# Dividing the inverse's PSUM copies of a delta-rule layer between ScalarE and VectorE

## The chip, the core and the metric

The kernel runs on one core of a Trainium2 chip, in one launch. The core has five engines that take their instructions strictly in order from a queue of their own: TensorE (PE in the profile, with its weight loads shown apart as PEld), VectorE (DVE), ScalarE (ACT), GpSimd (POOL) and SyncE (SP, which here only issues DMAs). Engines wait for each other by semaphores. The metric is the device time of the launch in microseconds (us); the kernel before takes 1310.35 us (median of 3 runs, 1309.5 to 1310.55).

## The reference: what is computed

The model is a two-layer encoder on 512 tokens of width 1024: layer 0 mixes tokens by a bidirectional gated delta rule (8 heads, keys and values of 128, chunks of 64 tokens), layer 1 by gated linear attention, and each is followed by a LayerNorm, an MLP with a squared ReLU and another LayerNorm. The change is in layer 0 alone. For each head, direction and chunk of 64 tokens the reference solves a triangular system:

```
kb = k * beta[..., None]
a_mat = where(strict, einsum('bhncd,bhnsd->bhncs', kb, k) * decay_mat, 0.0)
lhs = a_mat + eye(CHUNK)
sol = triangular_solve(lhs, rhs, lower=True, unit_diagonal=True)
u, w = sol[..., :dv], sol[..., dv:]
```

and then runs a recurrence over the chunks of the head (`v_new = u - w @ state`, output, new state), whose output is normed, gated and multiplied with the output weights.

## The kernel before, in words

The 512 tokens make four blocks of 128 (NT = 4), each holding two chunks; with two directions there are eight 128x128 matrices per head (U = 8). They are inverted all together, by joining blocks of growing size. `solve` (line 1593) first inverts 4x4 diagonal blocks, then walks through the sizes 4, 8, 16, 32 and 64. At each size there are three groups of eight float16 matmuls into PSUM tiles called `lv` (`prod`, line 1677): first ath by Dd (the off-diagonal blocks times the inverse so far); the result is copied, masked to the blocks in question, into the zeroed tile `pz` of that size; then Xd by pz, and pz by Xd, whose results update the inverse `Dd` and its transpose `Xd`. "Both factors" are these two. `d` counts the directions; a block of direction 0 and one of direction 1 lie in different rows (PSUM partitions) of the same `lv` tile, and one `lv` tile fills one PSUM bank. For sizes 4, 8 and 16 one VectorE product with a mask makes `pz`. For size 32 it is four ScalarE copies of 32x128 (line 1696). For size 64 `pz` is one ScalarE and one VectorE instruction (lines 1712 and 1710), and then two ScalarE copies write the last block of Dd (line 1717) and two VectorE copies the last block of Xd (line 1719).

After it one Newton step refines the inverse (tiles `nw`, lines 1728 to 1751), which gives `xf`. `recur` (line 1755) then runs the recurrence over four steps: matmul pairs `m` (line 1776) alternate with small ScalarE and VectorE instructions (tiles `r`, `vd`, `vn`, `sn`), and the head ends with 14 output matmuls `op` (line 1812). `finish` (line 1817) squares `op` on ScalarE (`junk`), makes a reciprocal root (`rsy`, `rst`, `ors`), scales (`fo`), transposes on TensorE (`otp`) and makes `p`, and its two halves `oh` and `ol`, the input of the output product.

Three heads are in work at once: the loop in `gdn` (line 1359) traces `recur` of head i-2, `solve` of head i-1, `project` of head i (96 matmuls of 512 columns, tiles `pjk`, `pjq`, `pjv`, `pjz`) and `finish` of head i-2. When no head is left to project, the output product of heads 0 to 5 (`out_pieces`, tiles `oa`, 144 matmuls of 512 columns) takes the projections' place, and `out_last` (line 315; tiles `ob`) adds heads 6 and 7: for each of four token blocks and two halves of the columns a product with the identity in full float32 (line 332) that brings in the residual, three matmuls for head 6 and three for head 7. When both halves of a block are complete, its LayerNorm (`layernorm`, line 223) runs on VectorE, and then its transposes (`tp`, line 190), which the first products of the MLP (`pj`) need.

The order in which these pieces stand in each engine's queue is not written by hand: the framework's scheduler puts them there when the program is built, by priority (mostly the order of the trace) and by its own estimate of what is ready at what time. It also sets the semaphores. So a change of a few copies can move instructions in all queues. `self.next.solved`, the last copy into Dd, is the instruction behind which the next head's exponentials `E` (line 1617) are allowed.

## Time and profile before

| | |
|---|---|
| median of 3 runs | 1310.35 us (1309.5 to 1310.55) |
| the profiled execution, its own time | 1310.2 us |
| its span (first to last instruction) | 1308.5 us |
| TensorE busy | 1289.2 us, 99% |
| VectorE busy | 1106.3 us, 85% |
| ScalarE busy | 804.4 us, 61% |
| granted TensorE clock | 0.996 |
| stage with the changed copies | from 60 to 363 us of the span (first and last of them at 73.8 and 363.3 us) |
| end of the last head's `op` matmuls | 383.5 us |
| LayerNorm of layer 0 and its transposes | to about 420 us |

A row of the timeline names the start, the duration, the engine, the line, the operation, the tiles (out<-in) and the shape, and in brackets the engine's idle time before it and who ended it. A matmul's duration is modelled and covers its pipeline, so what a matmul costs a busy TensorE is the distance between the starts of two matmuls that follow each other. A full-precision float32 matmul stands as two rows.

### The profile page before, as it was taken

The numbers are of one execution on the slowest core, as the hardware profiler recorded it, in microseconds if no ns is written. First come the engines' busy times: TensorE is split into PE (matmuls) and PEld (weight loads), VectorE is DVE, ScalarE is ACT, GpSimd is POOL, SyncE is SP. The second block draws the span as 40 slices with busy tenths as digits, with TensorE's granted clock in tenths as the row PEclk, the third lists the DMA queues.
The fourth block names the chain that finished last, engine by engine and source line by source line (L and its number), as shares of the span: only waits on it lengthen the run. The fifth ranks groups of instructions, "written<-read, shape, count | busy, mean of one in ns | idle before, by whom it ended". The sixth has DMA issues, their size and how long they took to land.

```text
span 1308.5 us, 22228 instructions
## 1 busy us (share of the span) xinstructions
PE 1289.2 (99%) x8586; PEld 1106.7 (85%) x8586; DVE 1106.3 (85%) x1795; ACT 804.4 (61%) x1604; POOL 134.5 (10%) x190
## 2 busy tenths in 40 slices
PE   8999999999999999999999999999999999999996
PEld 7778888888878899999998888888888899999985
DVE  7888887988868998999989697877888789989987
ACT  5767776677543656666657754564456566666656
POOL 5000000000003710101102100000001001101021
PEclk9999999999999999999999999999999999999998
DMA  5333313233332665566657421211317276556565
GB/s 192 98 107 97 98 57 107 81 114 104 107 113 82 177 175 167 122 198 162 179 146 156 136 97 62 68 64 50 107 54 228 78 210 164 144 176 139 170 143 144
DMA packets 47805, 165.92 MB, mean 127 GB/s; under 512 B 5923, under 2 KB 6611, under 8 KB 47699
## 3 DMA queue, kind: packets, MB, share of 16 engines
q1 hardware_dynamic: 33603, 114.52, 25.8%
q0 software_dynamic: 13984, 49.95, 18.8%
q8 instruction: 67, 1.10, 0.3%
q14 instruction: 39, 0.32, 0.1%
q10 hardware_dynamic: 112, 0.03, 0.0%
HBM read 125.00 MB, written 2.65 MB: 98 GB/s over the span
## 4 chain that ended last, share of the span: by engine, by line
PE 92%; DVE 3%; ACT 2%; DMA 1%; issue 1%; SPq 0%; DVEq 0%; ACTq 0%
PE pjv L128 3%; PE pjv L129 3%; PE pjv L130 3%; PE pX L130 3%; PE pX L129 3%; PE fx L130 3%; PE fx L128 3%; PE fx L129 3%; PE pX L128 3%; PE m L1776 3%; PE fyz L130 3%; PE fyz L128 3%; PE fyz L129 3%; PE pY L129 2%; PE pY L130 2%; PE pY L128 2%
## 5 line engine op out<-in xcount | busy, mean ns | idle before, releaser
L102 ACT CAST wh<-wst 128x1024 fp32r<-128x1024 f32 x151 | 158.5, 1050 | 104.6 <-PE fyz L129 28.3
L107 DVE TENSOR_TENSOR wl<-wst,wh 128x1024 fp32r<-128x1024 f32 x149 | 183.1, 1231 | 40.6 <-ACT wh L102 40.5
L107 DVE TENSOR_TENSOR w2l<-w2r,w2h 128x1024 fp32r<-128x1024 f32 x92 | 111.4, 1221 | 20.5 <-ACT w2h L102 20.5
L102 ACT CAST w2h<-w2r 128x1024 fp32r<-128x1024 f32 x94 | 98.4, 1048 | 41.5 <-DMA w2r<-w2r 22.9
L415 POOL DMA_DIRECT2D w2r<-w2r x56 | 47.9, 887 | 492.9 <-DVE w2l L107 387.7
L464 DVE TENSOR_TENSOR wst<-wst 128x512 f32<-128x512 f32 x120 | 79.9, 686 | 0.8
L102 ACT CAST ah<-h 128x1024 fp32r<-128x1024 f32 x56 | 58.8, 1050 | 30.6 <-PE pY L129 11.9
L107 DVE TENSOR_TENSOR al<-h,ah 128x1024 fp32r<-128x1024 f32 x56 | 68.3, 1220 | 6.6 <-ACT ah L102 6.6
L130 PE MATMUL pX<-w2h,al 128*128 128x512 f32 x168 | 66.3, 394 | 0.0
L129 PE MATMUL pX<-w2l,ah 128*128 128x512 f32 x168 | 65.9, 392 | 0.0
L128 PE MATMUL pX<-w2h,ah 128*128 128x512 f32 x168 | 65.4, 390 | 0.0
L128 PE MATMUL pjv<-wh,xth 128*128 128x512 f32 x128 | 54.7, 428 | 0.0
L130 PE MATMUL fyz<-xh,wl 128*128 128x256 f32 x192 | 53.5, 278 | 0.0
L130 PE MATMUL fx<-xth,wl 128*128 128x256 f32 x192 | 53.4, 278 | 0.0
L128 PE MATMUL fyz<-xh,wh 128*128 128x256 f32 x192 | 53.4, 278 | 0.0
L128 PE MATMUL fx<-xth,wh 128*128 128x256 f32 x192 | 53.2, 277 | 0.0
L130 PE MATMUL fx<-xh,wl 128*128 128x256 f32 x192 | 53.2, 277 | 0.0
L129 PE MATMUL fx<-xtl,wh 128*128 128x256 f32 x192 | 53.2, 277 | 0.0
L129 PE MATMUL fyz<-xl,wh 128*128 128x256 f32 x192 | 53.1, 277 | 0.0
L129 PE MATMUL fx<-xl,wh 128*128 128x256 f32 x192 | 53.1, 277 | 0.0
L128 PE MATMUL fx<-xh,wh 128*128 128x256 f32 x192 | 53.1, 277 | 0.0
L129 PE MATMUL pj<-xtl,wh 128*128 128x256 f32 (+1 forms) x160 | 52.0, 326 | 0.2 <-DVE xtl L194 0.2
(542 smaller groups left out, 4315.4 us busy)
## 6 DMA issues: line engine op xcount, KB each, us to landing
wst<-in_w SPq DMA_DIRECT2D x68, 512.0 KB, 4.8
w2r<-in_w SPq DMA_DIRECT2D x60, 512.0 KB, 4.5
w2r<-w2r POOLq DMA_DIRECT2D x56, 512.0 KB, 5.9
wst<-in_a_in SPq DMA_DIRECT2D x31, 512.0 KB, 3.8
wst<-in_b_vr SPq DMA_DIRECT2D x16, 512.0 KB, 3.3
wst<-in_a_out SPq DMA_DIRECT2D x8, 512.0 KB, 4.7
wst<-in_b_in SPq DMA_DIRECT2D x8, 512.0 KB, 3.4
wst<-in_b_out SPq DMA_DIRECT2D x8, 512.0 KB, 3.2
```

What stands on the lines that cost most here:

```text
L102: h = nc.scalar.copy(hi, src)
L107: self.halves = h, nc.vector.tensor_tensor(lo, src, hi.bitcast(F32), ALU.subtract)
L128: mm(ps, ah, bh, start=start, stop=False, **kw)
L129: mm(ps, ah, bl, start=False, stop=False, **kw)
L130: self.last_mm = mm(ps, al, bh, start=False, stop=stop, **kw)
L415: nc.gpsimd.dma_start(blocks[a + (q,)], blocks[b + (q,)], accum_op=ALU.add)
L464: plus = lambda a, b: V.tensor_tensor(a, a, b, ALU.add)
L1776: T.matmul(ps[:, d, :], *ops(d), start=True, stop=True)
```

## The change

At size 32 the two copies of direction 1 stay on ScalarE and the two of direction 0 go to VectorE. In the last block each factor gets one copy on each engine: Dd's direction 0 on ScalarE and direction 1 on VectorE, Xd's direction 0 on VectorE and direction 1 on ScalarE. Counted per head, the 32x128 copies are four on ScalarE before and two on each engine now; the 64x256 copies are two on each engine before and now, but in other pairs. `self.next.solved` becomes the first of the four, ScalarE's copy into Dd.

```
@@ -1693,8 +1693,9 @@
                 for d in (1, 0):
                     for b in range(2):
                         r0, c0 = 64 * b + s * (1 - d), 64 * b + s * d
-                        A.copy(pd[r0:r0 + s, dirs[d], c0:c0 + s],
-                               ps.rearrange("p d (n b) s -> p d n b s", n=NT)[r0:r0 + s, d, :, b, :])
+                        (A.copy if d else V.tensor_copy)(
+                            pd[r0:r0 + s, dirs[d], c0:c0 + s],
+                            ps.rearrange("p d (n b) s -> p d n b s", n=NT)[r0:r0 + s, d, :, b, :])
@@ -1713,10 +1714,11 @@
         ps = prod(xd, pd, 64, 0)
         px = prod(pd, xd, 64, 1)
-        for d in range(2):
-            self.next.solved = A.copy(dd[row(1 - d), dirs[d], row(d)], ps[row(1 - d), d, :, :])
-        for d in range(2):
-            V.tensor_copy(xd[row(d), dirs[d], row(1 - d)], px[row(d), d, :, :])
+        where = lambda t, i, d: (t[row(i), dirs[d], row(1 - i)], (px if t is xd else ps)[row(i), d, :, :])
+        self.next.solved = A.copy(*where(dd, 1, 0))
+        V.tensor_copy(*where(dd, 0, 1))
+        V.tensor_copy(*where(xd, 0, 0))
+        A.copy(*where(xd, 1, 1))
```

The new lines push what follows down by one or two: L1717 and L1719 of before are L1718 to L1721 now, L1728 is L1730, L1776 is L1778, L1812 is L1814, L1834 is L1836. The multiset of instructions stays the same but for the engine of these copies; the queues from about 430 us of the span on are the same. Three places show what moved. The semaphores that an instruction waits for stand in brackets.

The first place is VectorE's queue at the last block of head 7, the last head (Xd and Dd are the two factors, `a` is what the Newton step makes of `nw`, `z` the residual). Before:

```order
L1710 TENSOR_SCALAR pz_146<-lv 64x4x64 [waits Activation_49]
L311 SCALAR_TENSOR_TENSOR z<-z,oa 128x512 [waits DMAHW4_49,PE_49]
L1719 CAST Xd<-lv 64x4x64 [waits PE_49]
L1719 CAST Xd<-lv 64x4x64
L1840 SCALAR_TENSOR_TENSOR p<-otp,ng,sil 128x512 [waits PE_49]
```

Now:

```order
L1711 TENSOR_SCALAR pz_146<-lv 64x4x64 [waits Activation_49]
L1720 CAST Xd<-lv 64x4x64 [waits DVE_49,PE_49]
L1719 CAST Dd<-lv 64x4x64 [waits Activation_49]
L311 SCALAR_TENSOR_TENSOR z<-z,oa 128x512 [waits DMAHW7_49,PE_49]
L1732 SCALAR_TENSOR_TENSOR a_4969<-nw,Dd 128x512 [waits PE_49]
```

VectorE's copy into Dd waits for a ScalarE instruction ("Activation"), the copy into the other half of Dd, and stands behind the copy into Xd. The two copies at size 32 (L1696) on VectorE wait for ScalarE in the same way in all eight heads.

The second place is TensorE's queue in the last head's recurrence, from one `m` pair to the end of `op` and on to the first transpose of `finish`. Before (of the 14 `op` matmuls the first eleven are left out, and the `ob` groups that follow, up to `otp`, too):

```order
L1776 MATMUL m_5205<-r,xf 128x128 x2
L129 MATMUL oa<-wl,oh_340 128x512
L130 MATMUL oa<-wh,ol 128x512
L128 MATMUL oa<-wh,oh_340 128x512
L1776 MATMUL m_5216<-vd,kt 128x128 x2
...
L1812 MATMUL op<-vn,qke 128x128 x2
L1812 MATMUL op<-sn,qd 128x128
L129 MATMUL oa<-wl,oh_341 128x512
L130 MATMUL oa<-wh,ol 128x512
L128 MATMUL oa<-wh,oh_342 128x512
```

Now:

```order
L1778 MATMUL m_5205<-r,xf 128x128 x2
L332 MATMUL ob<-z,ident 128x512
L1778 MATMUL m_5216<-vd,kt 128x128 x2
...
L1814 MATMUL op<-vn,qke 128x128 x2
L1814 MATMUL op<-sn,qd 128x128
L128 MATMUL ob<-oah,oh_343 128x512
L129 MATMUL ob<-oal,oh_343 128x512
L130 MATMUL ob<-oah,ol 128x512
L1836 MATMUL otp<-ident,fo 128x128 x4
L128 MATMUL ob<-oah,oh_343 128x512
```

The `oa` matmuls that stood between the `m` pairs are used up, and pieces of `ob` stand there. Before, 8 `oa` matmuls, three `ob` products with the identity and 6 other `ob` matmuls stand between the last `op` and the first `otp`; now 3 `ob` matmuls. Counted over the whole stage, 880 of the 888 matmuls of 512 columns (projections and `oa`) stood ahead of the end of the last head's `op`, and none of `ob`; now all 888 do, and five products with the identity and 12 other `ob` matmuls. Changes from a group of float16 matmuls to one of 512 columns number 107 before and 118 now, up to the first `tp`.

The third place is ScalarE's queue behind the last head's recurrence (`vn` its last values, `junk` the squares of `op`, `wh` halves of the MLP's weights, `rsy` and `fo` as above). Before:

```order
L1794 ACTIVATE vn<-m_5230 128x128 x2
L1824 ACTIVATE junk,oss<-op 128x128 x2
L102 CAST wh<-wst 128x1024
L1824 ACTIVATE junk,oss<-op 128x128
L102 CAST wh<-wst 128x1024
L1824 ACTIVATE junk,oss<-op 128x128
L202 ACTIVATE rsy<-oss,bias_77 128x4
```

Now:

```order
L1796 ACTIVATE vn<-m_5230 128x128 x2
L1826 ACTIVATE junk,oss<-op 128x128 x4
L202 ACTIVATE rsy<-oss,bias_77 128x4
L203 ACTIVATE rsy<-rsy 128x4
L1832 ACTIVATE fo<-op,ors 128x128 x4
```

Two weight casts that stood between the squares now stand ahead of `vn`, and VectorE's subtractions that go with them likewise.

## The prediction

> **What bounds the kernel now.** I read the first part of the page first, then the copies by tile, then the timeline around them.

> ```profile
> span 1308.5 us, 22228 instructions
> PE 1289.2 (99%) x8586; PEld 1106.7 (85%) x8586; DVE 1106.3 (85%) x1795; ACT 804.4 (61%) x1604; POOL 134.5 (10%) x190
> ```

> TensorE is busy for 99% of the span. A copy on another engine can cost or save time only where TensorE waits for it, or where it changes what TensorE has left to do while it waits for something else. The view of the `lv` tile gives the copies (minimum/median/maximum in ns, first and last start):

> ```profile
> L1696 ACT CAST pz<-lv x32: 247/256/258, 73.8 to 359.0; 32x128 f16<-32x128 f32 x32
> L1717 ACT CAST Dd<-lv x16: 365/366/367, 78.9 to 363.1; 64x256 f16<-64x256 f32 x16
> L1719 DVE CAST Xd<-lv x16: 407/422/428, 79.7 to 363.3; 64x256 f16<-64x256 f32 x16
> ```

> Around the first head's copies the timeline (start, duration, engine, work) shows how much of them TensorE sees:

> ```profile
> 73.76 1.07 ACT L1696 CAST pz<-lv 32x128 f16<-32x128 f32 x4 [1.33 <-PE lv L1682]
> 73.78 0.48 PE L129 MATMUL pjk<-xtl,wh 128*128 128x512 f32 x1
> 74.10 0.40 PE L130 MATMUL pjk<-xth,wl 128*128 128x512 f32 x1
> 74.46 0.48 PE L128 MATMUL pjk<-xth,wh 128*128 128x512 f32 x1
> 74.88 0.28 PE L1682 MATMUL lv<-pz,Xd 128*128 128x64 f16 x4
> 78.87 0.76 ACT L1717 CAST Dd<-lv 64x256 f16<-64x256 f32 x2 [0.96 <-PE lv L1682]
> 79.21 0.40 PE L130 MATMUL pjq<-xth,wl 128*128 128x512 f32 x1
> 79.68 0.22 PE L1728 MATMUL nw<-Dd,ath 128*128 128x128 f16 x1
> ```

> While ScalarE makes its four copies (1.07 us), TensorE multiplies for the projections. A matmul of 512 columns occupies it for 0.23 us (383.80 to 384.03 in the rows further down), so the product at 74.88, 0.42 behind its forerunner, waited 0.19 us for `pz`; the one at 79.68, 0.47 behind, waited 0.24 us for Dd. Of this kind there are six waits for the first (1.2 us in all) and eight for the second (2.0 us). All that faster copies could give is these **3.2 us**; everything else of ScalarE's 14.1 us of copies (32 by 0.256 and 16 by 0.366) is hidden behind projections, and later `oa`.

> **The copies themselves.** Two of four small copies and one of two large ones change engine. VectorE's 32x128 cast is not in the trace. It lies between ScalarE's own 0.256 us and VectorE's 64x256 at 0.422; the work is a quarter, so I take a value near the lower end, 0.29. For the 64x256 copies both engines have rows: 0.366 and 0.422. If both engines worked side by side, four copies of 1.07 us would become two by 0.29, and the waits above would vanish: −3.2 us. But the program as built makes VectorE's copy wait for ScalarE's, since both read the same `lv` tile. Whether such a wait costs its full length, the kernel before shows in size 64, where `pz` is already divided in just this way:

> ```profile
> 361.12 0.38 ACT L1712 ACTIVATE pz<-lv 64x256 f16<-64x256 f32 x1 [1.85 <-PE lv L1682]
> 361.53 0.42 DVE L1710 TENSOR_SCALAR pz<-lv 64x256 f16<-64x256 f32 x1
> ```

> VectorE begins 0.03 us after ScalarE's end: one behind the other, never together. By that, two ScalarE copies and then two on VectorE take about 0.53 + 0.03 + 0.58 = 1.14 us, against 1.07: no gain, +0.07. At the last block a gain is left: Dd's first copy on ScalarE and Xd's on VectorE read different tiles, so the two engines overlap across the factors, and both factors are done in about 0.85 us instead of 0.37 × 2 for Dd and then 0.87 from 79.73 for Xd. Dd, which `nw` needs, is complete after 0.37 + 0.03 + 0.42 = 0.82 instead of 0.76 (+0.06), unless VectorE is held in Xd's copy. The eight waits for Dd I count as staying or going by what stands ahead of them in TensorE's queue: where fillers are moved there, they go. The whole sum of waits removed is taken as −2.0, between 0 and −3.2.

> [...]

> **What waits behind the wait.** VectorE takes its queue in order, so in each head two of its new copies hold it until ScalarE is done: 16 times, 0.3 to 0.5 us by the durations above, 5 to 8 us of VectorE over a stage of 300 us in which it is 85% busy (page). What queues behind (the V casts, `ktp`, the residual) feeds TensorE with some slack; the order has also 11 more changes from float16 to 512 columns (107 to 118), and the first matmul after such a change takes 0.32 instead of 0.23 us (383.48 to 383.80 to 384.03): 11 × 0.09 = +1.0. For the shorter covers of `pz` at size 64 and `ktp` I add +0.9, an estimate from five places with 0.2 us each, as in the wait at 74.88. Together with −2.0: **−0.1**, between −3.2 and +2.

> **The order, where the money lies.** With the inverse later in the plan, the `oa` matmuls are used up early. In the last head TensorE has 8 more of them, 5 products with the identity and 12 other `ob` ahead of the last `op`. What stood behind `op` before:

> ```profile
> 383.34 0.39 PE L1812 MATMUL op<-sn,qd 128*128 128x128 f32 x2
> 383.48 0.48 PE L129 MATMUL oa<-wl,oh 128*128 128x512 f32 x1
> 383.80 0.39 PE L130 MATMUL oa<-wh,ol 128*128 128x512 f32 x1
> 384.03 0.39 PE L128 MATMUL oa<-wh,oh 128*128 128x512 f32 x1
> ...
> 385.41 1.02 PE L332 MATMUL ob<-sil,ident 128*128 128x512 f32 x2
> 385.87 0.79 PE L128 MATMUL ob<-oah,oh 128*128 128x512 f32 x1
> 386.50 0.39 PE L129 MATMUL ob<-oal,oh 128*128 128x512 f32 x1
> ...
> 389.66 0.33 PE L1834 MATMUL otp<-ident,fo 128*128 128x128 f32 x1
> ...
> 391.79 0.50 PE L128 MATMUL ob<-oah,oh 128*128 128x512 f32 x1
> ```

> An identity product with the matmul behind it spans 385.41 to 386.50, so the product itself is 1.09 − 0.23 = 0.86. Moved ahead of the end of `op`: 8 × 0.23 + 5 × 0.86 + 12 × 0.23 = 1.84 + 4.30 + 2.76 = **8.9 us**; the last `op` ends about 8.9 − 0.1 = 8.8 us later. That alone would be no loss, since what went ahead is not to be done behind. It is a loss as far as the stretch behind is bound by something else than TensorE, and it is: `finish` needs ScalarE and VectorE before `otp`, and after `oh` the LayerNorm needs VectorE.

> ```profile
> 384.43 1.04 ACT L102 CAST wh<-wst 128x1024 fp32r<-128x1024 f32 x1
> 385.63 1.04 ACT L102 CAST wh<-wst 128x1024 fp32r<-128x1024 f32 x1
> 387.31 1.22 DVE L107 TENSOR_TENSOR wl<-wst,wh 128x1024 fp32r<-128x1024 f32 x1
> 387.76 0.21 ACT L203 ACTIVATE rsy<-rsy 128x4 f32<-128x4 f32 x1
> 388.45 0.15 DVE L204 TENSOR_TENSOR rst<-rsy 128x4 f32<-128x4 f32 x1
> ```

> From the last `op` (383.48) to `otp` (389.66) the chain took 6.18 us. The two casts stood between the squares and held it by about 0.95 each (1.04 less the overlap of its ends), and the subtraction at 387.31 held `rst` by 0.4 (388.45, where 0.21 after 387.76 would be about 388.0). Both stand earlier now: 6.2 − 1.9 − 0.4 = 3.9. From there to the first `ob` with the new `oh` 391.79 − 389.66 = 2.13. Then the LayerNorm; the stretches from there (their columns: window, length, then busy time of PE, PEld, DVE, ACT and POOL with counts):

> ```profile
> 395.00:400.00 5.00, 5.00 (x22) 3.47 (x21) 4.97 (x13) 1.20 (x5) 0.00 (x0) 1.00 0.00 0
> 400.00:405.00 5.00, 5.00 (x23) 3.19 (x23) 4.87 (x11) 1.34 (x3) 0.00 (x0) 1.00 0.00 0
> 405.00:410.00 5.00, 5.00 (x40) 4.73 (x39) 4.84 (x15) 1.80 (x6) 0.00 (x0) 1.00 0.02 5
> ```

> VectorE is at 97 to 99% here, and TensorE too: before, both just balanced. VectorE's chain does not get shorter, whatever TensorE has done ahead. It runs from 391.79 to the transposes of the third token block:

> ```profile
> 411.05 0.28 PE L129 MATMUL pj<-xtl,wh 128*128 128x256 f32 x1
> 411.17 0.28 PE L130 MATMUL pj<-xth,wl 128*128 128x256 f32 x1
> 411.31 0.63 PE L190 MATMUL tp<-ident,xt 128*128 128x128 f32 x4
> ```

> 411.31 − 391.79 = 19.5. So from the last `op` to that `tp`: 3.9 + 2.1 + 19.5 = 25.5 us, where it was 411.31 − 383.48 = 27.8: **−2.3**. TensorE has work for only 18 or 19 us of it (27.8 less the 8.9 moved ahead) and idles for about 7. At the end five more `pj` matmuls stand behind that `tp` than before, each 0.12 (411.05 to 411.17): +0.6.

> **The sum:** +8.9 − 0.1 − 2.3 + 0.6 = **+7.1 us**. Against the profiled execution's 1310.2 that is 1317.3; the median of the runs, 1310.35, is 0.15 above, so I say **1317.3**. If the finish chain does not lose its 2.3, +9.4; if waits go by the full 3.2 and the late fillers by a third less, +2.

> **The rivals.** B, the copies run side by side, the waits of 3.2 us vanish, and the tail costs nothing for C's reason. For it: different rows of the tile; against it: 361.12 and 361.53, the built waits, and what speaks against C. Time 1310.2 − 3.2 = 1307.0. C, the work is only moved: TensorE finds in the tail all the work that it found before, and only the −0.1 counts, 1310.1. For it: 99% busy, and a planner that looks at the whole; against it: VectorE at 4.97 of 5.00 in the tail, which work on TensorE cannot shorten. D, VectorE becomes the bound already in the stage: it waits 16 times up to 0.5 us in order, and what stands behind it (`ktp`, V's casts, the products with masks) comes late for TensorE by that much in two cases of three: +5.3 on top of 7.1, 1322.6. It decides once VectorE's slack in a head is under a us; at 85% of some 35 us a head it has about 5, which speaks against it.

> [...]

> **How the numbers follow.** My forecast has 0.72, B 0.07, C 0.11, D 0.10. A measurement of this kernel can tell 0.2%, 2.6 us, from no change. Faster is B alone (1307.0 is 3.35 below the median): 0.07. No change is C and the lowest part of the forecast, 0.13. Slower is the rest, 0.80. The range takes in C and ends short of D: 1310.0 to 1321.0, which leaves out B and D, 0.17; the forecast's own would be 1312 to 1320.

> **What would show it.** Right, if the last `op` ends near 392 us, `otp` follows it by about 4 us instead of 6.2, TensorE idles for about 7 us between 395 and 420 with VectorE at 95% or more, and everything from `pj` on lies some 7 us later at unchanged distances. The copies: VectorE's 32x128 near 0.29 us, beginning when ScalarE's end. Wrong, if they overlap (B), if TensorE is as busy in the tail as before (C), or if it loses time before 370 us behind VectorE (D).

## The result, and the profile after

The changed kernel takes 1322.33 us (median of 5 runs, 1321.16 to 1324.91) against 1309.89 us of the kernel before (median of 5, 1309.5 to 1310.55): a ratio of 1.0095, 95% interval 1.0083 to 1.0106. It is slower, as forecast, but by 12.4 us and not by 7.1, above the range. The page of its profiled execution:

```profile
span 1320.6 us, 22210 instructions
PE 1295.3 (98%) x8586; PEld 1109.4 (84%) x8586; DVE 1111.3 (84%) x1811; ACT 802.8 (61%) x1588; POOL 134.4 (10%) x190
```

The span is 12.1 us longer, and TensorE is now idle for 25 us of it (19 before). The tile view of `lv` (minimum/median/maximum in ns) gives the divided copies:

```profile
L1696 ACT CAST pz<-lv x16: 255/256/258, 73.4 to 364.7; 32x128 f16<-32x128 f32 x16
L1696 DVE CAST pz<-lv x16: 283/290/297, 74.4 to 365.9; 32x128 f16<-32x128 f32 x16
L1718 ACT CAST Dd<-lv x8: 367/368/368, 78.4 to 369.9; 64x256 f16<-64x256 f32 x8
L1719 DVE CAST Dd<-lv x8: 406/407/409, 79.4 to 370.5; 64x256 f16<-64x256 f32 x8
```

The durations are what the prediction took (0.29 for the small cast). When the copies run is another matter. The first head in the timeline, ScalarE, VectorE and TensorE apart:

```profile
73.36 0.52 ACT L1696 CAST pz<-lv 32x128 f16<-32x128 f32 x2 [1.34 <-PE lv L1682]
78.38 0.37 ACT L1718 CAST Dd<-lv 64x256 f16<-64x256 f32 x1 [1.33 <-PE lv L1682]
78.77 2.16 ACT L1617 ACTIVATE E<-E,cj 128x128 f32<-128x128 f32 x7
80.96 0.37 ACT L1721 CAST Xd<-lv 64x256 f16<-64x256 f32 x1
```

```profile
73.67 0.69 DVE L1610 TENSOR_TENSOR on<-kk,nd 128x512 f32<-128x512 f32 x1 [0.23 <-PE kk L1602]
74.37 0.59 DVE L1696 CAST pz<-lv 32x128 f16<-32x128 f32 x2
78.25 1.21 DVE L107 TENSOR_TENSOR wl<-wst,wh 128x1024 fp32r<-128x1024 f32 x1
79.39 0.41 DVE L1719 CAST Dd<-lv 64x256 f16<-64x256 f32 x1
```

```profile
80.36 0.23 PE L1730 MATMUL nw<-Dd,ath 128*128 128x128 f16 x1
```

ScalarE is done with its pair of size 32 at 73.88, but VectorE is in another instruction until 74.36 and begins its pair only then. In the last block ScalarE's half of Dd is ready at 78.75, but VectorE has just begun a weight subtraction of 1.21 us and copies its half from 79.39 on. And ScalarE's half of Xd stands behind seven exponentials of the next head, which the first copy into Dd lets in now. From the starts and ends of these rows in all eight heads (means of eight): Dd is complete 0.76 us after its first copy began in the kernel before, and 1.05 now (0.83 to 1.56); the first `nw` follows 0.05 us behind that before, and 0.36 now, because TensorE's queue has been arranged for a later Dd and has other matmuls there: in seven of eight heads TensorE waited for Dd ahead of the first `nw` before, and in none now. The four copies of size 32 take 1.07 us before and 1.36 now, and the product that needs the last of them follows 0.06 behind before and 0.46 now.

The last inverse comes late. The end of the last head in TensorE's timeline of the changed kernel:

```profile
382.70 0.40 PE L130 MATMUL ob<-ol 128*128 128x512 f32 x1
384.53 0.75 PE L1778 MATMUL m<-vd,kt 128*128 128x128 f32 x4 [1.43 <-ACT vd L1793]
...
394.34 0.39 PE L1814 MATMUL op<-sn,qd 128*128 128x128 f32 x2
...
395.03 0.40 PE L130 MATMUL ob<-oah,ol 128*128 128x512 f32 x1
398.34 1.25 PE L1836 MATMUL otp<-ident,fo 128*128 128x128 f32 x4 [2.92 <-ACT fo L1832]
400.60 0.79 PE L128 MATMUL ob<-oah,oh 128*128 128x512 f32 x1 [1.01 <-ACT oh L1843]
401.19 0.63 PE L129 MATMUL ob<-oal,oh 128*128 128x512 f32 x1
401.62 0.63 PE L130 MATMUL ob<-oah,ol 128*128 128x512 f32 x1
...
422.26 0.63 PE L190 MATMUL tp<-ident,xt 128*128 128x128 f32 x4
```

ScalarE's rows at the wait of 384.53:

```profile
383.16 1.04 ACT L102 CAST wh<-wst 128x1024 fp32r<-128x1024 f32 x1 [3.60 <-DMA wst<-in_w]
384.11 0.62 ACT L1793 ACTIVATE vd<-m,kds 128x128 f32<-128x128 f32 x2
```

A cast of an MLP weight waited for its DMA, the recurrence's `vd` stood behind it, and TensorE waited for `vd`. And a thing that the prediction has not at all: at 401.19 and 401.62 the distance of two `ob` matmuls is 0.43 us, not 0.23. The windows (length; PE busy first, the granted clock third from the end) show why:

```profile
395.00:398.00 3.00, 0.42 (x2) 0.00 (x0) 0.85 (x6) 1.82 (x11) 0.00 (x0) 1.00 0.00 0
398.00:399.00 1.00, 0.66 (x3) 0.42 (x3) 0.00 (x0) 1.00 (x4) 0.00 (x0) 0.95 0.00 0
399.00:400.00 1.00, 0.59 (x2) 0.22 (x2) 0.37 (x1) 0.06 (x1) 0.00 (x0) 0.50 0.00 0
400.00:405.00 5.00, 4.40 (x10) 3.47 (x11) 2.88 (x7) 0.80 (x2) 0.00 (x0) 0.50 0.00 0
405.00:406.00 1.00, 1.00 (x4) 0.83 (x3) 0.65 (x2) 0.29 (x1) 0.00 (x0) 0.64 0.00 0
406.00:407.00 1.00, 0.67 (x3) 0.19 (x2) 0.99 (x2) 0.20 (x1) 0.00 (x0) 1.00 0.00 0
```

TensorE was idle from 395.4 to 398.3; from 398.9 to about 405.7 its granted clock is half. VectorE is not full there (2.88 of the 5 us from 400 to 405), so it is not what bounds this stretch.

The account of the 12.1 us, from the starts of four matmuls in both traces (last `nw`, last `op`, first `otp`, first `tp` of the third token block): the last `nw` is 7.3 us later (368.37 to 375.63); from there to the last `op` it takes 3.7 us more (15.1 to 18.8); to `otp` 2.3 less (6.2 to 3.9); to the `tp` 2.3 more (21.7 to 23.9). That is 10.95; the five `pj` left over add 0.7. From 425 to 1290 us of the span the delay stays at 11.6 us; the last 0.5 comes in the last 20 us.

What TensorE does up to the last `op`, before and now (window, length, then PE's busy time first):

```profile
60.00:383.45 323.45, 321.43 (x2897) 263.67 (x2897) 267.63 (x537) 215.08 (x623) 12.05 (x18) 1.00 0.31 94
60.00:394.45 334.45, 331.49 (x2922) 269.33 (x2919) 276.12 (x557) 215.14 (x608) 12.05 (x18) 1.00 0.32 97
```

Of the 11.0 us by which the last `op` is later, 10.1 are busy time of TensorE and 0.9 idle time. It hardly waits for the late copies: it does other work meanwhile, and that is the work that now stands ahead of the last inverse and of `op`.

### The profile page after: what moved, and what is told of

Read it like the earlier page. It is cut to its first block, busy times and chain, and to the rows that moved or that the text cites. A ratio compares the mean times of both kernels' runs of the same rounds, so it can differ in the third digit from the quotient of the medians.

```text
span 1320.6 us, 22210 instructions
## 1 busy us (share of the span) xinstructions
PE 1295.3 (98%) x8586; PEld 1109.4 (84%) x8586; DVE 1111.3 (84%) x1811; ACT 802.8 (61%) x1588; POOL 134.4 (10%) x190
## 3 DMA queue, kind: packets, MB, share of 16 engines
q1 hardware_dynamic: 33603, 114.52, 25.4%
## 4 chain that ended last, share of the span: by engine, by line
PE 91%; DVE 4%; ACT 3%; DMA 1%; issue 1%; SPq 0%; DVEq 0%; ACTq 0%
PE pjv L128 3%; PE pjv L130 3%; PE pjv L129 3%; PE pX L130 3%; PE pX L129 3%; PE fx L130 3%; PE fx L128 3%; PE fx L129 3%; PE pX L128 3%; PE m L1778 3%; PE fyz L128 3%; PE fyz L130 3%; PE fyz L129 2%; PE pY L129 2%; PE pY L130 2%; PE pY L128 2%
## 5 line engine op out<-in xcount | busy, mean ns | idle before, releaser
L102 ACT CAST wh<-wst 128x1024 fp32r<-128x1024 f32 x151 | 158.3, 1049 | 111.5 <-PE fyz L129 28.1
L107 DVE TENSOR_TENSOR wl<-wst,wh 128x1024 fp32r<-128x1024 f32 x149 | 183.4, 1232 | 42.0 <-ACT wh L102 41.9
L107 DVE TENSOR_TENSOR w2l<-w2r,w2h 128x1024 fp32r<-128x1024 f32 x92 | 111.7, 1225 | 22.0 <-ACT w2h L102 22.0
L102 ACT CAST w2h<-w2r 128x1024 fp32r<-128x1024 f32 x94 | 98.4, 1048 | 41.5 <-DMA w2r<-w2r 22.7
L102 ACT CAST ah<-h 128x1024 fp32r<-128x1024 f32 x56 | 58.8, 1051 | 30.6 <-PE pY L129 12.1
L107 DVE TENSOR_TENSOR al<-h,ah 128x1024 fp32r<-128x1024 f32 x56 | 68.5, 1223 | 6.6 <-ACT ah L102 6.6
L130 PE MATMUL pX<-w2h,al 128*128 128x512 f32 x168 | 66.3, 394 | 0.0
L129 PE MATMUL pX<-w2l,ah 128*128 128x512 f32 x168 | 65.9, 392 | 0.0
L128 PE MATMUL pX<-w2h,ah 128*128 128x512 f32 x168 | 65.4, 390 | 0.0
L128 PE MATMUL pjv<-wh,xth 128*128 128x512 f32 x128 | 54.8, 428 | 0.0
L130 PE MATMUL fyz<-xh,wl 128*128 128x256 f32 x192 | 53.5, 278 | 0.0
L130 PE MATMUL fx<-xth,wl 128*128 128x256 f32 x192 | 53.4, 278 | 0.0
L128 PE MATMUL fyz<-xh,wh 128*128 128x256 f32 x192 | 53.4, 278 | 0.0
L128 PE MATMUL fx<-xth,wh 128*128 128x256 f32 x192 | 53.2, 277 | 0.0
L130 PE MATMUL fx<-xh,wl 128*128 128x256 f32 x192 | 53.2, 277 | 0.0
L129 PE MATMUL fx<-xtl,wh 128*128 128x256 f32 x192 | 53.1, 277 | 0.0
L129 PE MATMUL fyz<-xl,wh 128*128 128x256 f32 x192 | 53.1, 277 | 0.0
L129 PE MATMUL fx<-xl,wh 128*128 128x256 f32 x192 | 53.1, 277 | 0.0
L128 PE MATMUL fx<-xh,wh 128*128 128x256 f32 x192 | 53.1, 277 | 0.0
L129 PE MATMUL pj<-xtl,wh 128*128 128x256 f32 (+1 forms) x160 | 52.0, 326 | 0.2 <-DVE xtl L194 0.2
```

The costliest lines, as they stand in the source:

```text
L102: h = nc.scalar.copy(hi, src)
L107: self.halves = h, nc.vector.tensor_tensor(lo, src, hi.bitcast(F32), ALU.subtract)
L128: mm(ps, ah, bh, start=start, stop=False, **kw)
L129: mm(ps, ah, bl, start=False, stop=False, **kw)
L130: self.last_mm = mm(ps, al, bh, start=False, stop=stop, **kw)
```

## The experiments

Two theories to start with. **O**: the loss is in the order of the last head's tail. **V**: VectorE's part of the copies comes late in every head. For the clock there was **K**: the idle time halved it. Of each run the table gives, after all of them, where its trace stood.

**One weight cast out of the way.**

```
-        self.ahead = [self.wcols(w, i * P, at=64) for i in range(n)]
+        self.ahead = [self.wcols(w, i * P, late=late if i == n - 1 else (), at=64) for i in range(n)]
```

(`late` is the last `vn` copy of head 7.)

> The changed kernel with one weight cast of the MLP (and the subtraction that belongs to it) queued behind the last values `vn` of the last head's recurrence, and not ahead of its second `vd`; all other queues are the same, word for word. Theory O (the loss is the order in the last head): TensorE's wait of 1.6 us at 382.70 goes, and 1322.3 falls by 1.2 to 1.6 us, to about 1320.8. Theory V (the divided copies themselves cost it, by VectorE's waits all along the stage): no change, 1322.3.

Measured 1320.73 us (1320.31 to 1321.09), 1.6 less. In TensorE's timeline the wait is gone, and the matmul follows its forerunner without a pause:

```profile
383.37 0.40 PE L130 MATMUL ob<-ol 128*128 128x512 f32 x1
383.61 0.67 PE L1778 MATMUL m<-vd,kt 128*128 128x128 f32 x4
```

So 1.6 us of the 3.7 between `nw` and `op` were this cast. A part of the rest is the longer work between the `m` pairs: two steps with a product with the identity in one and three `ob` in the other take 2.59 us in the changed kernel (384.53 to 387.12), where three `oa` in each made it 2.40 before (375.06 to 377.46).

**Idle transposes in the first hole.**

```
-        for n in range(NT):
-            T.transpose(otp[:, n, :], on[:, n, :], c.ident)
+        with c.in_order(mybir.EngineType.PE):
+            if self.h == A_H - 1:
+                idle = self.bank("idle", tag="tp")
+                with c.tc.issue_after(self.op_last.ins):
+                    for n in range(24):
+                        T.transpose(idle[:, n % NT, :], c.ident, c.ident)
+            for n in range(NT):
+                T.transpose(otp[:, n, :], on[:, n, :], c.ident)
```

> The changed kernel with 24 idle transposes (2.6 us of TensorE, result unused) right behind the last `op`, where TensorE idled for 3.1 us until `otp`. Theory K (the granted clock fell to 0.50 from 398.9 to 405.6 us because of that idle time, and the 12 `ob` matmuls that ran at 0.43 instead of 0.23 us set the end): the clock stays at 1.00, 2.1 us come back, 1320.2. Rival (the LayerNorm on VectorE sets the end whatever the clock): no change, 1322.3. Rival (the transposes hold `otp` back): slower, up to 1323.

Measured 1324.94 us (1322.65 to 1326.24): not faster; the range overlaps that of the changed kernel. Its profiled execution (1325.45 us) shows the clock falling at two places, neither of them the hole that was filled:

```profile
384.00:386.00 2.00, 0.80 (x5) 0.78 (x6) 1.09 (x1) 1.74 (x5) 0.00 (x0) 1.00 0.36 145
386.00:390.00 4.00, 4.00 (x14) 3.00 (x13) 1.26 (x5) 0.00 (x0) 0.00 (x0) 0.57 0.39 135
390.00:400.00 10.00, 10.00 (x74) 8.37 (x72) 1.94 (x10) 3.38 (x16) 0.00 (x0) 1.00 0.00 0
400.00:403.00 3.00, 1.46 (x7) 0.96 (x7) 1.33 (x4) 1.90 (x6) 0.00 (x0) 1.00 0.00 0
403.00:406.70 3.70, 3.70 (x11) 2.77 (x10) 2.17 (x5) 0.04 (x1) 0.00 (x0) 0.55 0.00 0
```

The first fall follows the wait for the weight cast, which is longer in this execution than in the other, where the clock held (1.43 us, and 1.00 from 384 to 390 us):

```profile
385.20 0.75 PE L1778 MATMUL m<-vd,kt 128*128 128x128 f32 x4 [1.88 <-ACT vd L1793]
```

The second follows two holes around `otp`, of 0.5 and 1.0 us. The filled hole itself (390 to 400) is at full clock, and `otp` was not held back (3.9 us behind `op`, as in the changed kernel). So one hole filled is not enough, and a hole of 1.9 us can do it. The falls differ between executions: the fastest of the four had a mean clock of 0.997, like the kernel before, and still took 1322.65 us, not the 1320.2 that K expects. That left K open until all the holes were filled at once:

**Both holes filled, and the cast out of the way.** As above, with 34 transposes ahead of `otp` and 10 behind it, on top of the late cast.

> The late-cast kernel (1320.7) with idle transposes, result unused, in both holes of TensorE behind the last `op`: 34 (3.6 us) ahead of `otp` and 10 (1.1 us) behind it. Theory K (TensorE's clock is halved when it has been idle for about 2 us of a few): the clock stays at 1.00 up to 420 us, the `ob` matmuls run at 0.23 us, 2.1 us come back less 0.7 for three `ob` that stand behind `otp` now: 1319.3. Rival (the fall of the clock has another cause, or VectorE sets the end): 1320.7 or more.

```profile
396.00:400.00 4.00, 4.00 (x28) 3.13 (x27) 2.14 (x7) 1.94 (x6) 0.00 (x0) 1.00 0.00 0
400.00:404.00 4.00, 3.94 (x17) 2.81 (x16) 3.92 (x8) 0.50 (x2) 0.00 (x0) 1.00 0.00 0
```

The clock holds, and from `otp` to the third block's `tp` it takes 21.5 us, where the kernel with the late cast alone had 23.7. K holds for the clock and for the tail. But the time is 1320.41 us (1319.29 to 1321.02), not measurably under 1320.73. In its profile the 2.2 us are lost again later: at the third block's `tp` it is 7.1 us behind the kernel before, at 720 us 9.4, and 10.2 at the end of layer 1. TensorE waits for ScalarE there, which is held by weight casts, as at 580 us (`h`, `fx` and `fyz` are tiles of that later stage; ScalarE's rows, then TensorE's):

```profile
579.46 1.04 ACT L102 CAST wh<-wst 128x1024 fp32r<-128x1024 f32 x1
580.40 0.37 ACT L523 ACTIVATE h<-fx 128x256 f32<-128x256 f32 x1
```

```profile
580.00 0.28 PE L130 MATMUL fx<-xth,wl 128*128 128x256 f32 x1
580.83 0.38 PE L128 MATMUL fyz<-xth,wh 128*128 128x256 f32 x1 [0.55 <-ACT h L523]
```

The kernel with the late cast alone has no such waits between 440 and 720 us. So in this kernel the fall of the clock costs the tail 2.2 us and the whole nothing measurable: with the clock held, the gain is lost later. What these casts wait for was not followed.

**Cover put back behind `op`.**

```
+            held = behind is not None and t == NT - 1 and i >= len(ks) - 3
+            with self.tc.issue_after(behind.ins) if held else contextlib.nullcontext():
+                self.mm3(ps, ah, al, wh[:, i % 2, :], wl[:, i % 2, :], i == 0, i == len(ks) - 1)
```

(in `out_pieces`; `out_last` holds all of `ob` likewise. `behind` is the last `op` matmul of head 7.)

> The changed kernel, but the last nine `oa` matmuls and all of `ob` are held behind the last head's last `op`, so that 9 `oa`, 3 products with the identity and 6 other `ob` cover the way from `op` to `otp` again, as before the change. Theory O: nothing stands between the `m` pairs then, the chain runs at its own pace (11.7 us from the first `m` to `op` before), `op` ends 3.3 us earlier, the clock does not fall: about 1318.9, 1317 to 1320. Theory V: no change, 1322.3.

Measured 1322.00 us (1321.73 to 1322.88): nothing gained. The windows of its trace, from the first `m` pairs to `op`:

```profile
376.00:380.00 4.00, 2.44 (x12) 1.67 (x12) 2.29 (x4) 2.47 (x8) 1.09 (x2) 1.00 0.49 162
380.00:382.00 2.00, 1.51 (x6) 1.22 (x7) 0.23 (x1) 0.88 (x4) 0.00 (x0) 0.56 0.72 277
386.00:394.00 8.00, 6.50 (x28) 5.79 (x27) 1.21 (x4) 1.40 (x6) 0.00 (x0) 0.51 0.01 2
```

The tail was as before the change (`op` to `otp` 6.3 us, on to `tp` 21.7), but with nothing between the `m` pairs TensorE was busy for only about 60% of a stretch of 4 us (376 to 380), with no single wait over half a microsecond, and its clock fell. At half clock an `m` step takes 1.6 to 1.8 us, against 1.2 before the change, and what was gained behind `op` was lost ahead of it.

**The same with idle transposes between the `m` pairs**, six behind each pair of head 7.

> The kernel with `oa` and `ob` held behind the last `op` (1322.0), with six idle transposes (0.65 us, result unused) behind each of the last head's ten `m` pairs, where TensorE sat idle and its clock was 0.50 from about 381 to 394 us. Theory K: the clock stays at 1.00, an `m` step takes 1.2 us again and not 1.7 (nine of them: 4.3 us), `op` 3.1 us again (1.6 us less): 5.9 us back, 1316.1. Rival (the chain over ScalarE and VectorE sets the pace, whatever the clock): 1322.

Measured 1320.18 us (1320.02 to 1320.97). The clock, with the same stretch in view:

```profile
380.00:384.00 4.00, 4.00 (x36) 3.81 (x35) 1.60 (x6) 0.96 (x4) 0.00 (x0) 1.00 0.36 139
384.00:388.00 4.00, 4.00 (x34) 3.78 (x34) 1.28 (x5) 0.96 (x4) 0.00 (x0) 1.00 0.00 0
```

At full clock `nw` to `op` takes 15.8 us, with only idle transposes between the `m` pairs, against 19.7 at half clock: 3.9 us for the clock alone, of the 5.9 expected. A part is given back in the MLP again (8.5 us behind the kernel before at `tp`, 9.6 at 720 us). The tail is repaired now in each of its parts (`nw` to `op`, `op` to `otp`, `otp` to `tp` are within 0.8 us of the kernel before), and the kernel is still 10 us slower. What stays is the lateness of the last inverse, 7.6 us in this execution. Theory O explains the smaller part.

**Which copies make it late.** Four runs with a part of the change each, then two with the exponentials let in later.

Only size 32 divided:

> Only the copies at size 32 divided, the last block as before. By the queues, 8 `oa` and one product with the identity less stand behind the last `op` (2.7 us of TensorE; with both edits 8.9 us). Theory O (the loss goes with the work used up ahead of the last `op`): 2 to 4 us over the kernel before, 1312 to 1314. Rival (one of the edits carries the whole loss): 1310 or 1322.

Measured 1310.32 us (1309.95 to 1311.52; ratio 1.000, interval 0.9991 to 1.001): no measurable loss and below theory O's range, though 2.7 us of TensorE's work moved ahead of `op`. Only the last block divided:

> Only the last block's copies divided, size 32 as before. By the queues 8 `oa`, two products with the identity and 3 other `ob` less stand behind the last `op` (4.3 us). Theory O: 3 to 6 us over the kernel before, 1313 to 1316. Rival (one of the edits carries the whole loss): 1310 or 1322.

Measured 1315.97 us (1314.81 to 1316.44). It falls in the range, but the run before has taken its reason away. The rival of the one edit that carries everything is out too: 0.4 and 6.0 don't add up to 12.4, so the two together cost more than their sum.

Of the last block, only Dd divided, or only Xd:

```
         self.next.solved = A.copy(*where(dd, 1, 0))
         V.tensor_copy(*where(dd, 0, 1))
         V.tensor_copy(*where(xd, 0, 0))
-        A.copy(*where(xd, 1, 1))
+        V.tensor_copy(*where(xd, 1, 1))
```

> Only the last block, and of it only Dd divided: ScalarE makes one half of Dd, VectorE the other and both halves of Xd; ScalarE has no copy behind the exponentials. Theory X: no loss, 1309 to 1312. Theory V: as with both divided, 1314 to 1317.

```
+        A.copy(*where(dd, 1, 0))
+        self.next.solved = A.copy(*where(dd, 0, 1))
+        V.tensor_copy(*where(xd, 0, 0))
+        A.copy(*where(xd, 1, 1))
```

> Only the last block, and of it only Xd divided: ScalarE makes both halves of Dd as before and one half of Xd, which stands behind one or two of the next head's exponentials (0.3 to 0.6 us), VectorE the other half of Xd. Theory X: a part of the loss, 1311 to 1316. Theory V: no loss, 1309 to 1311.

Dd alone: 1315.61 us (1314.92 to 1316.68). Xd alone: 1312.61 (1312.05 to 1314.69). VectorE's half of Dd costs what both together cost; V has the larger part. The half of Xd costs something too (its time lies in X's range and above V's). Head 4 with only Dd divided, ScalarE's row, VectorE's and then TensorE's:

```profile
242.37 0.37 ACT L1717 CAST Dd<-lv 64x256 f16<-64x256 f32 x1 [1.35 <-PE lv L1682]
```

```profile
241.54 1.21 DVE L107 TENSOR_TENSOR wl<-wst,wh 128x1024 fp32r<-128x1024 f32 x1
242.77 0.42 DVE L1718 CAST Dd<-lv 64x256 f16<-64x256 f32 x1
```

```profile
242.17 0.40 PE L1682 MATMUL lv<-Xd,pz 128*128 128x64 f16 x8
...
243.64 0.23 PE L1729 MATMUL nw<-Dd,ath 128*128 128x128 f16 x1
```

Dd is complete at 243.19, and `nw` comes 0.45 us behind it. In this head VectorE is not held: its weight subtraction ends at 242.75, when ScalarE's half is done (242.74), and Dd takes 0.82 us, as the prediction has it. The lateness is TensorE's queue alone. In four of the eight heads of this kernel VectorE is held as well, by 0.2 to 0.5 us. With Xd alone divided Dd is complete 0.76 us after its first copy began and `nw` follows by 0.05, in all eight heads, as before the change.

With the exponentials let in behind ScalarE's second copy (only the last block divided, then the whole change):

```
-        self.next.solved = A.copy(*where(dd, 1, 0))
+        A.copy(*where(dd, 1, 0))
...
-        A.copy(*where(xd, 1, 1))
+        self.next.solved = A.copy(*where(xd, 1, 1))
```

> Only the last block divided (1316.0), but the next head's exponentials `E` are let in behind ScalarE's second copy (the half of Xd), not behind its first. In the kernels measured so far up to seven exponentials of 0.31 us stand between ScalarE's two copies. Theory X (that delay of Xd's half is what makes the inverses late): the 6 us go, 1309 to 1312. Theory V (VectorE's copy of the half of Dd, behind other work in VectorE's queue, makes them late): 1316.

> The whole change (1322.3) with `E` let in behind ScalarE's second copy of the last block. Theory X: the loss goes, 1310 to 1313. Theory V, and theory Q (the two edits together make the inverses late whatever the exponentials do; by the queues there is hardly more behind the last `op` than in the change): 1320 to 1322.

Measured 1314.34 us (1313.58 to 1317.69) and 1318.59 us (1317.86 to 1319.79): 1.6 and 3.7 us better than without (the ranges of the first pair overlap, those of the second don't). In the whole change the exponentials ahead of Xd's half are a part of it; neither theory has its number.

**Does lateness add up over the heads?** The change in head 7 alone, and in all heads but head 7 (by a condition on `h` around both edits):

> The whole change in the last head alone, heads 0 to 6 as before. Theory A (lateness is handed on from head to head: in the changed kernel the last `nw` of head 6 comes 4.6 us late and that of head 7 7.3 us): only what the last head adds itself, 0 to 3 us, 1310 to 1313. Theory B (what the last head does with its own copies decides, since only there nothing is left to fill TensorE): 6 us or more, 1316 and up.

> The whole change in heads 0 to 6, the last head as before. Theory A: most of the loss stays, 1317 to 1321. Theory B: the loss goes, 1310 to 1313.

Measured 1310.62 us (ratio 1.0006, interval 0.9997 to 1.0015) and 1320.57 us (1320.43 to 1320.82). Alone, the last head's own copies cost nothing measurable, and on top of the others' some 2 us; what the heads ahead of it hand on costs nearly everything. Theory A. It is not handed on evenly, though: in the changed kernel the last `nw` of the eight heads comes 0.5, 1.2, 1.3, 3.6, 3.2, 1.3, 4.6 and 7.3 us later than before, so it also falls back between heads.

**One copy made twice, in the kernel before** (`r0`, `c0`, `b` and `d` have the values of the loop's last copy).

```
+            if s == 32:
+                A.copy(pd[r0:r0 + s, dirs[d], c0:c0 + s],
+                       ps.rearrange("p d (n b) s -> p d n b s", n=NT)[r0:r0 + s, d, :, b, :])
```

> The kernel before with one of ScalarE's four copies at size 32 made twice in every head: 0.26 us more between two products of each inverse, with the filler matmuls where they were. Theory O: only the waits for `pz` grow, by at most 8 times 0.26: 1310 to 1312. Theory V (lateness of the copies is itself what costs): it adds up along the chain of heads, more than 1312.

Measured 1314.97 us (1314.34 to 1316.49): 5.3 us for 2.1 us of copies, with all on ScalarE and the tail's cover as before. My remark that the fillers stay where they were holds for the tail alone; ahead of it the queues came out otherwise, and TensorE does wait here: from 60 to 340 us it is idle for 3.7 us, against 1.2 in the kernel before and in the change. So a later copy on ScalarE can cost more than its length as well.

**The change with a higher priority for VectorE's copies** when the queues are put in order (size 32, and its half of Dd).

> The whole change, with a higher priority for VectorE's copies at size 32 and its half of Dd when the queues are put in order. By the queues 2.7 us of work are moved ahead of the last `op`, as with size 32 alone, and not 8.9. Theory O: the time follows what is moved ahead: 1310 to 1312. Theory L (it follows the lateness of the last inverse, which VectorE's half of Dd causes, and a priority cannot stop what VectorE has begun): 1314 to 1320.

Measured 1313.85 us (1313.36 to 1314.84): just under the lower end of theory L's range, and well over O's. As much work is moved ahead of `op` here as with size 32 alone, which cost nothing.

All the kernels, by the starts in their traces (last `nw`; from there to the last `op`, to the first `otp`, to the first `tp` of the third block; us) and their medians:

| kernel | last `nw` | to `op` | to `otp` | to `tp` | median |
|---|---|---|---|---|---|
| before | 368.4 | 15.1 | 6.2 | 21.7 | 1309.9 |
| only size 32 | 367.8 | 16.9 | 4.3 | 21.8 | 1310.3 |
| head 7 alone | 368.8 | 16.3 | 4.3 | 21.8 | 1310.6 |
| only Xd | 370.4 | 16.5 | 3.9 | 21.6 | 1312.6 |
| last block, `E` later | 371.7 | 15.2 | 6.6 | 21.7 | 1314.3 |
| priority | 371.8 | 16.6 | 3.9 | 21.8 | 1313.9 |
| one copy twice | 372.4 | 15.2 | 6.2 | 21.7 | 1315.0 |
| only Dd | 372.7 | 15.8 | 3.9 | 22.5 | 1315.6 |
| whole, `E` later | 373.3 | 17.8 | 3.9 | 23.8 | 1318.6 |
| last block | 374.0 | 16.7 | 3.9 | 21.6 | 1316.0 |
| all heads but 7 | 374.1 | 19.1 | 3.9 | 23.9 | 1320.6 |
| whole change | 375.6 | 18.8 | 3.9 | 23.9 | 1322.3 |
| cover put back | 375.8 | 19.7 | 6.3 | 21.7 | 1322.0 |
| first hole filled | 375.8 | 20.8 | 3.9 | 23.0 | 1324.9 |
| both holes filled, late cast | 375.9 | 17.1 | 3.9 | 21.5 | 1320.4 |
| cover put back, transposes | 375.9 | 15.8 | 6.3 | 21.7 | 1320.2 |
| late cast | 376.3 | 17.1 | 3.9 | 23.7 | 1320.7 |

In the first twelve rows the time follows the first column: taken off the median's excess over 1309.9, the lateness of the last `nw` (its excess over 368.4) leaves 0.3 to 1.4 us in the eight with at most 22.5 in the fourth column (for the last block alone the clock is 1.00 from 390 to 402 us, for one copy twice from 365 to 440). In the three with 23.8 or 23.9 there it leaves 3.8 to 5.2 us; in two of them the windows show the clock's fall (0.50 in the whole change, 0.54 from 395 to 399 us with `E` later). The last five rows keep the lateness and change the tail. There it leaves 2.7 and 3.0 us even in the two whose clock was held (1.00 from 372 to 424 us); of these, 1.0 and 2.4 us were lost only behind 425 us of the span.

## Why the prediction was wrong

The direction, the place (the last head's tail), the work moved ahead and the idle TensorE were right. The size was not: +12.4 against +7.1.

- **The step that failed** is the term "from the last `op` to that `tp`: −2.3"; it measured 0.0. `op` to `otp` took 3.9 us, to the tenth. But I took VectorE's 19.5 us as the bound whatever TensorE does, and TensorE idled, its clock fell to half, and the `ob` matmuls of 0.43 us became the bound: +2.3 from `otp` to `tp`, so that the sum is zero. VectorE, which I had expected at 95% or more from 395 to 420 us, was busy for 18.3 of these 25 us. With the clock held (both holes filled) the stretch takes 25.4 us, where the forecast has 25.5, though the whole kernel then loses the difference later. My forecast idled TensorE for seven microseconds and didn't ask what that does to its clock. In the traces the clock went to 0.50 behind an idle stretch of 2.9 us here, behind one of 1.9 us with the first hole filled, and, with the cover put back, behind 4 us in which TensorE was busy for 61% without a wait over half a microsecond.
- **The last `op`**, estimated 8.8 us later, came 11.0 later. The work moved ahead, 8.9 us, is there: TensorE's busy time up to the last `op` grew by 10.1 us (with the changes of group, which I had priced at 1.0). What the sum doesn't have is the wait for `vd` behind a weight cast, 1.6 us; I had read the moved casts only as a relief for `finish`. These two steps are 3.9 of the 5.3 us that the forecast lacks.
- **The copies** themselves were mis-sized too. I set four copies of size 32 at +0.07 us and Dd at +0.06, by the row in which VectorE begins 0.03 us behind ScalarE. That is right where VectorE is free (1.15 us for size 32 in four of eight heads, 0.83 to 0.86 for Dd in three). In the others VectorE is in something else: for Dd in a weight subtraction in two heads (0.6 and 0.8 us lost), in another instruction in one, and in its own copy of Xd, which stands ahead, in the rest (0.2 us each). I asked what waits behind VectorE's copies and not what they wait behind. On the mean Dd is complete 0.29 us later per head and size 32 likewise, and TensorE's queue brings the next product another 0.31 and 0.40 us later. That is 1.3 us per head; the stretch from the first `xp` (the transposes of Dd that give Xd) to the first `nw` of an inverse grew by more, from 20.1 to 22.5 us (mean of eight), and the rest was not followed. In the sum this has no term of its own: the lateness of the last inverse, 7.3 us, and the work moved ahead, which I read from the queues, are two sides of one thing, since TensorE does that work while the inverse is late. What is moved ahead does not set the time alone: with 2.7 us of it the time was the same (size 32), 0.5 over (head 7 alone) or 3.8 over (priority).
- **+0.6 for the left-over `pj`** was 0.7, and 0.5 us more came at the end of the kernel, which has no term.
- **B and C** are out: ScalarE's and VectorE's copies of one tile don't overlap (of each pair that the change divides, the later begins 0.02 to 0.83 us behind the earlier one's end, in all eight heads; whether they could run together without the waits that the program has for them no run shows), and the tail does not absorb it. **D** gave 1322.6, near the measured time by luck: from 60 to 340 us TensorE is busy for 278.8 of 280 us in both kernels. (A modelled duration can hide a wait of 0.2 us, as in the prediction's first rows. As an estimate, the distances between starts, each less the usual one for the same two kinds of matmul, add up to 0.5 us more in that stretch than before, not to D's 5.3.) VectorE's load does enter, by making the copies late.

Open: why half a microsecond a head costs nothing at size 32 alone (the copies are done 0.34 us later, and the product comes another 0.21 later) and over 5 us with Dd alone (0.20 and 0.31). The queues are put in order anew in each of these kernels, and I have no run that keeps them fixed and changes the copies alone. A cause for the last 0.5 us was not looked for.

## What to carry to other kernels

Before a copy on a serial chain goes to another engine, read in the timeline what that engine is in the middle of when the copy's input is ready: where the fuller engine is busy, its unfinished instruction is added to the chain (here up to 0.8 us, and in some heads nothing). In a pipeline that is full everywhere but at its end, such lateness need not show as a wait anywhere: other work goes ahead, and is missing as cover at the end. Here the change in seven heads cost 10.5 us and in the last one alone nothing measurable. It is not the delay per head times the heads (half a microsecond a head cost nothing at size 32 alone), so each part has to be measured. And where a change leaves TensorE idle for two or three microseconds, the matmuls behind the hole should be priced at half clock too: here those of 512 columns took 0.43 us instead of 0.23 behind a hole of 2.9 us, while one of 2.0 us in the kernel before left the clock at 1.00.
